# Third up-projection block: where its gate weights are loaded, when the SiLU table is loaded, and where the gating stands in the order

## The chip, the cores and the metric

The kernel runs on one core of one Trainium2 chip. A core has TensorE (PE; its weight loads are shown as PEld), VectorE (DVE), ScalarE (ACT), GpSimd (POOL) and SyncE (SP), which issues most DMAs. Each engine runs its own instructions in order and waits on semaphores for the others. The metric is the device time in microseconds of one execution, as the median of several runs; lower is better.

## The reference

One transformer-like layer on 1024 latent tokens of width 1024 with 256 context tokens: modulated RMSNorm, one input projection, retention and differential attention side by side, one output projection with a gated residual, then the part that matters here:

```python
h2 = rms_norm(x, norm2_g) * (1.0 + sc2) + sh2
x = x + g2 * conv_ffn(h2, w_up, conv_w, conv_b, w_down)

def conv_ffn(h, w_up, conv_w, conv_b, w_down):
    u = h @ w_up                                   # (1024, 2 * 2816)
    up = jnp.pad(u, ((0, 0), (1, 1), (0, 0)))
    u = up[:, :-2] * conv_w[0] + up[:, 1:-1] * conv_w[1] + up[:, 2:] * conv_w[2] + conv_b
    a, b = jnp.split(u, 2, axis=-1)
    return (jax.nn.silu(a) * b) @ w_down
```

## The kernel before, in words

All matrix products are made in float32 of about full precision: each operand is split into a high and a low part (`split_op`, L916: ACT casts the high part `whi` at L919, DVE subtracts to get the low part `wlo` at L920), and each 128x128x512 product is three matmuls, high x high (L129), high x low (L130) and low x high (L131).

The hidden width 2816 is worked off in 22 blocks of 128 columns (`NF`). Block j needs two weight blocks, `w_up[j]` (tile `wra`, the part that goes through the SiLU) and `w_up[j + 22]` (tile `wrb`, the gate weights), each 512 KB. The two weight blocks and the tokens form a 2x2 block product by a Strassen-like scheme with seven products, p1 to p7, of 12 matmuls each. POOL forms the sums of weight blocks (`combined`, L1064: L1074 adds two halves of `wrb`, L1075 to L1077 go on with `wra`), and the sums of activations, `B11`, `B21`, `B22`, `T1` to `T4`, are kept in SBUF. Some results are running sums in one PSUM bank, `chain`: p1, then p6 is added and ACT copies the bank (L1161), then p7 is added and ACT copies it (L1169), then p4 is added and ACT copies it (L1177). TensorE can't add the next product to the bank before the copy is made.

The order of the work around the change:

- In the output projection (L993 to L1018) `norm2` (L949) stores each of the 8 tiles `x1[t]`, sums its squares on ACT (L952), takes the power on POOL (`rsqrt`, L115) and scales the tile on DVE (L954). After it the tiles are turned by TensorE (`turned`, L959) and split into the activations; `turned1` (L1030) does the second half of the tokens and the sums beside the first products of the up-projection, and uses x1[4] to x1[7] for the last time.
- Products that need no sum of all activations come first (L1084 to L1099): p1 and p2 of blocks 0 to 2 (`NPRE`), p5 and p3 of blocks 0 and 1 (`NSUM`; the weight sums of these two blocks are made in place earlier).
- Then the main loop (L1187). In round j it loads the weights of block j + 1 (from block 3 on), calls `begin` (p1 and p2, or what is there of them), `end` of block j - 1 (p3 and p4), `gated` of block j - 1, and `middle` of block j (p6, p5, p7). `gated` (L1179) makes the width-3 convolution of both halves (`conv`, L1109: one ACT step at L1112 and two DVE steps at L1113 and L1114 each), the SiLU on ACT (L1182), the product with the gate on DVE (L1183) and the sums and stores for the down-projection (`down_operands`, L1121).
- Block 2 is the first whose weights are loaded in this part: `up_load(2)` (L977, called at L1118) loads `wrb` into a tile of its own, `third_b`, which takes memory over what `raw0` and the scratch tiles of `turned1` held, and then `wra` into one of the two buffers that the loads share. `in_order` (L117) fixes the order of the two.
- A scheduler orders the instructions of each engine by their place in the program and by when it reckons them ready; `add_manual_dep` with NoSync fixes an order between two instructions of one engine and adds no semaphore. A tile's memory is given on when all accesses to it are done.

The table of the SiLU is loaded by an instruction that the compiler puts ahead of the first activation that needs it.

Of the kernel before, what the change touches and what calls it, by code (L numbers as in the profile page):

```python
# [8 lines left out]
F32 = mybir.dt.float32  # L9
F32R = mybir.dt.float32r  # L10
BF16 = mybir.dt.bfloat16
AF = mybir.ActivationFunctionType
# [5 lines left out]
P = 128  # L18
D = 1024
KD = D // P  # L20
L = 1024
NT = L // P
# [6 lines left out]
NF = DFF // P  # L29
# [43 lines left out]
def kernel(  # L73
# [16 lines left out]
    nc = tc.nc  # L90
# [22 lines left out]
    def rsqrt(out_ap, in_ap, mul, eps, n):  # L113
        nc.vector.tensor_scalar(out=out_ap, in0=in_ap, scalar1=mul, scalar2=eps, op0=ALU.mult, op1=ALU.add)  # L114
        nc.gpsimd.tensor_tensor(out=out_ap, in0=out_ap, in1=mhalf[:, :n], op=ALU.pow)  # L115

    def in_order(start):  # L117
        last = {}
        for ins in nc.cur_bb.bb.instructions[start:]:
            if ins.engine not in FORCE:  # L120
                continue
            if ins.engine in last:
                tc.add_manual_dep(ins, last[ins.engine].name, mybir.DependencyInfo(mybir.DependencyClass.NoSync, mybir.DependencyReason.DATA), reason="order")
            last[ins.engine] = ins

    def passes(ps, lt, rt, first, last, more=False):
# [25 lines left out]
    with ExitStack() as p1:  # L152
# [217 lines left out]
        side = {"g": iter(()), "rate": 0.0, "due": 0.0}  # L370
# [7 lines left out]
        def beside(g, rate, due=0.0):  # L378
            for _ in side["g"]:
                pass  # L380
            side.update(g=g, rate=rate, due=due)
# [115 lines left out]
        with ExitStack() as p0:  # L497
# [92 lines left out]
            for i in range(2):  # L590
                for q in range(2):
                    t = 2 * i + q
# [287 lines left out]
    with ExitStack() as p2:  # L880
# [3 lines left out]
        start = len(nc.cur_bb.bb.instructions)  # L884
        order = sorted(TAU.items(), key=lambda it: it[1] % 1.0)
        for n in range(n_units + 8):
# [6 lines left out]
            if n in (8, 10, 12, 14):  # L893
                a, i = divmod(n // 2 - 4, 2)
# [8 lines left out]
            if n + 3 < n_units:  # L903
                after = units[n - 5].pool_ins if n >= 5 else last_va[0]
# [7 lines left out]
    wst = ctx_r.enter_context(tc.tile_pool(name="wst", bufs=2, side="right"))  # L912
# [7 lines left out]
        nc.vector.tensor_tensor(out=lo, in0=src, in1=r32(hi), op=ALU.subtract)  # L920
        return hi, lo

    def raw_load(name, src, pool=None):
        o = (pool or wst).tile([P, KD, P], F32, name=name)
        nc.sync.dma_start(out=o, in_=src)
        return o

    def product(ps, op, tt, first):
        hi, lo = op
        for k in range(4):  # L930
            passes(ps, (hi[:, k, :], lo[:, k, :]), (tt[0][:, k, :], tt[1][:, k, :]), first and k == 0, k == 3, not first)
            tick()

    B11, B21, B22, T1 = [tuple(yT[a][i][:, c : c + 4, :] for a in range(2)) for i, c in ((0, 0), (0, 4), (1, 0), (1, 4))]
    rawp = ExitStack()
    x1hp = rawp.enter_context(tc.tile_pool(name="x1h", bufs=1, side="right"))
    rwp = rawp.enter_context(tc.tile_pool(name="rwp", bufs=1, side="right"))
# [2 lines left out]
    x1lS = ExitStack()  # L940
    x1lp = x1lS.enter_context(tc.tile_pool(name="x1l", bufs=1, side="right"))
    xo = x1lS.enter_context(tc.tile_pool(name="xo", bufs=1, side="right"))
    x1 = [(x1lp if t < 4 else x1hp).tile([P, D], F32, name=f"x1_{t}") for t in range(NT)]
    raw0 = rwp.tile([P, KD, 512], F32, name="raw0")
    sm2 = rwp.tile([P, 64], F32, name="sm2")
    for t in range(NT):
# [2 lines left out]
    def norm2(t):  # L949
        nc.sync.dma_start(out=x1_d[t], in_=x1[t])  # L950
        sq = xo.tile([P, D], BF16, name="sq2")
        nc.scalar.activation(sq, x1[t], AF.Square, accum_out=sm2[:, t : t + 1])  # L952
        rsqrt(sm2[:, t : t + 1], sm2[:, t : t + 1], 1.0 / D, EPS, 1)
        nc.vector.tensor_scalar(out=x1[t], in0=x1[t], scalar1=sm2[:, t : t + 1], scalar2=None, op0=ALU.mult)  # L954

    def turned(hf, d, raw, on_act):
# [19 lines left out]
    NSUM = 2  # L976
    def up_load(j):  # L977
        if j == NSUM:
            start = len(nc.cur_bb.bb.instructions)
            b = raw_load("wrb", w_up[j + NF], third_b)  # L980
            a = raw_load("wra", w_up[j])
            in_order(start)
            return a, b
        return raw_load("wra", w_up[j]), raw_load("wrb", w_up[j + NF])

    def sums_in_place(a, b):
# [6 lines left out]
    with ExitStack() as p3:  # L993
        ps = p3.enter_context(tc.tile_pool(name="ps3", bufs=2, space=PSUM))
        for n in range(2):
# [3 lines left out]
            for t in range(NT):  # L999
# [5 lines left out]
                gated = wo.tile([P, 512], F32, name="gated")  # L1005
                nc.vector.tensor_tensor(out=gated, in0=pt, in1=g1[:, n * 512 : (n + 1) * 512], op=ALU.mult)
                nc.vector.tensor_tensor(out=dst, in0=gated, in1=dst, op=ALU.add)
                if n == 1:
                    norm2(t)
                    if t == 1:  # L1010
                        pre = [raw_load("wra" if j < 2 else "wrb", w_up[j]) for j in range(NPRE)]
                        early = [[split_op(a[:, c : c + 4, :]) for c in (0, 4)] for a in pre]
                        raws = [up_load(j) for j in range(NSUM)]
# [41 lines left out]
    def bank(name, pool=None):  # L1055
        return (next(bank_cycle) if pool is None else pool).tile([P, 512], F32, name=name, tag="bank")
# [40 lines left out]
    for j, pool in enumerate((psB, psC)):  # L1097
        third[j] = bank("third", pool)
        product(third[j], split_ahead[NSUM + j], B22, True)  # L1099
    beside(iter(()), 0.0)  # L1100
    tmpS.close()
    rawp.close()
    bank_cycle = itertools.cycle([psC] * 2 + [psB] * 2 + [psA] * 4)
# [2 lines left out]
    with ExitStack() as p4:  # L1106
        up = p4.enter_context(tc.tile_pool(name="up", bufs=2, side="right", reuse_waits="tile"))

        def conv(u, idx):  # L1109
            w = [cl[:, COL_CW + i * 44 + idx : COL_CW + i * 44 + idx + 1] for i in range(3)]  # L1110
            t = up.tile([P, L], F32, name="tconv", bufs=4)
            nc.scalar.activation(t, u, AF.Identity, scale=w[1], bias=cl[:, COL_CB + idx : COL_CB + idx + 1])  # L1112
            nc.vector.scalar_tensor_tensor(out=t[:, 1:], in0=u[:, : L - 1], scalar=w[0], in1=t[:, 1:], op0=ALU.mult, op1=ALU.add)  # L1113
            nc.vector.scalar_tensor_tensor(out=t[:, : L - 1], in0=u[:, 1:], scalar=w[2], in1=t[:, : L - 1], op0=ALU.mult, op1=ALU.add)  # L1114
            return t

        third_b = p4.enter_context(tc.tile_pool(name="third_b", bufs=1, side="right", reuse_waits="tile"))
        raws.append(up_load(NSUM))  # L1118
        held = {}

        def down_operands(j, g):  # L1121
            m, odd = divmod(j, 2)
            lo, hi = g[:, :512], g[:, 512:]
            eng = nc.gpsimd if j >= NF - 2 else nc.sync
            eng.dma_start(out=a_d[0][m][:, odd, :], in_=lo)
            if not odd:
                s34 = up.tile([P, 2, 512], F32, name="s34", bufs=1)
                nc.vector.tensor_tensor(out=s34[:, 0, :], in0=lo, in1=hi, op=ALU.subtract)
                held.update(lo=lo, hi=hi, s34=s34)
                return  # L1130
            eng.dma_start(out=a_d[3][m // 2][:, m % 2, :], in_=hi)
            s21 = up.tile([P, 2, 512], F32, name="s21", bufs=1)
            nc.vector.tensor_tensor(out=s21[:, 1, :], in0=held["hi"], in1=hi, op=ALU.add)
            nc.vector.tensor_tensor(out=s21[:, 0, :], in0=s21[:, 1, :], in1=held["lo"], op=ALU.subtract)
            eng.dma_start(out=a_d[1][m], in_=s21)
            nc.vector.tensor_tensor(out=held["s34"][:, 1, :], in0=lo, in1=s21[:, 0, :], op=ALU.subtract)
            eng.dma_start(out=a_d[2][m], in_=held["s34"])

        class Block:
# [18 lines left out]
            def middle(self):  # L1158
                j = self.j
                product(self.chain, self.op("p6"), T2, False)  # L1160
                nc.scalar.copy(self.ua[:, 512:], self.chain)  # L1161
                if j < NSUM:
                    self.third, self.fifth = third[j], fifth[j]
                    nc.vector.tensor_tensor(out=self.ua[:, 512:], in0=self.fifth, in1=self.ua[:, 512:], op=ALU.add)
                else:
                    self.third = self.fifth = bank("third")
                    product(self.third, self.op("p5"), T1, True)
                product(self.chain, self.op("p7"), T3, False)
                nc.scalar.copy(self.ub[:, 512:], self.chain)  # L1169
                nc.vector.tensor_tensor(out=self.ub[:, 512:], in0=self.fifth, in1=self.ub[:, 512:], op=ALU.add)  # L1170
# [5 lines left out]
                nc.vector.tensor_tensor(out=self.ua[:, 512:], in0=self.third, in1=self.ua[:, 512:], op=ALU.add)  # L1176
                nc.scalar.copy(self.ub[:, :512], self.chain)  # L1177

            def gated(self):  # L1179
                ta = conv(self.ua, self.j)  # L1180
                tb = conv(self.ub, self.j + NF)
                nc.scalar.activation(ta, ta, AF.Silu)  # L1182
                nc.vector.tensor_tensor(out=ta, in0=ta, in1=tb, op=ALU.mult)  # L1183
                down_operands(self.j, ta)

        last = None
        for j in range(NF):  # L1187
            if NSUM < j + 1 < NF:
                raws.append(up_load(j + 1))
            blk = Block(j)  # L1190
            blk.begin()
            if last is not None:
                last.end()
                last.gated()
            blk.middle()
            last = blk
        last.end()

# [6 lines left out]
        def split1(src):  # L1205
            hi, lo = split_op(src.rearrange("p (a b) -> p a b", b=P))
            return flat(hi), flat(lo)

        def step(pd, a, b, first, last, more=False, ts=range(4)):
            for t in ts:  # L1210
                passes(pd[t], tuple(g[:, t * P : (t + 1) * P] for g in a), b, first, last, more)
# [3 lines left out]
        for m in range(2):  # L1215
# [5 lines left out]
            for i, cc in enumerate((c1, c2)):  # L1221
                step(cc, split1(pa[:, i * C : (i + 1) * C]), split1(pb[:, i * C : (i + 1) * C]), m == 0, False)
        last.gated()
    ctx_t.close()
    ctx_y.close()
    ctx_ya.close()
# [218 lines left out]
```

## Time and profile before

| | |
|---|---|
| median of 3 runs | 1414.38 us (1412.52 to 1414.53) |
| span of the profiled execution, first to last instruction | 1413.6 us (the page gives no other time of it) |
| TensorE busy | 1372.1 us, 97% of the span |
| DVE busy | 991.1 us, 70% |
| ACT busy | 729.1 us, 52% |
| POOL busy | 286.1 us, 20% |
| mean granted TensorE clock | 0.992 |
| TensorE waits between 740 and 860 us | 4.6 us in three waits |

Times in the rows are microseconds from the span's start. A timeline row has the start, the duration, the engine, the line, the operation, output<-inputs, the shape and a count; brackets at its end hold the idle time of the engine ahead of it and what ended that idle time. In the table of windows each row has the stretch, its length, and the busy time with the number of instructions of PE, PEld, DVE, ACT and POOL, then the granted clock of TensorE (1.00 is full speed), the share of time that the DMA engines were busy, and GB/s. A row of waits has who waited for whom, the total, how often, and the longest. The up-projection runs from about 760 to 1190 us.

### The profile page before, as it was taken

To read this page: it belongs to the slowest core of one execution; us is meant where nothing else is said; L and a number is where in the kernel's file an instruction comes from. 1 tells how busy PE (TensorE), PEld (TensorE's weight loads), DVE (VectorE), ACT (ScalarE), POOL (GpSimd) and SP (SyncE) were. 2 spreads that over 40 slices of the span, in tenths; PEclk is the share of its full clock that TensorE was granted. 3 is DMA by queue.
4 is the path that set the end of the run, shared out by engine and by line. 5 is a ranking of instruction groups with operands and counts; after the bars stand their busy time and mean duration, and the time that the engine had idled before them with its cause. 6 is when DMAs were issued, how large, how long until landed. Compare 5 with 4: busy or idle time off the path is not lost.

```text
span 1413.6 us, 19193 instructions
## 1 busy us (share of the span) xinstructions
PE 1372.1 (97%) x6924; PEld 1141.8 (81%) x6924; DVE 991.1 (70%) x1433; ACT 729.1 (52%) x1386; POOL 286.1 (20%) x321
## 2 busy tenths in 40 slices
PE   6999999999999999999999999999999999999996
PEld 2588888888888799998888778888888888888885
DVE  3464965334586798896357888877788777898457
ACT  3453312333565689997126645554455555455533
POOL 1220000000556133411201232233322220000001
PEclk8999999999999999999999999999999999999999
DMA  8645886365474796631421223223233226953224
GB/s 305 228 135 179 280 293 202 116 201 183 149 246 159 196 220 153 128 79 62 163 82 60 90 105 112 92 109 112 97 112 112 81 84 221 393 180 105 90 97 178
DMA packets 96662, 218.79 MB, mean 155 GB/s; under 512 B 9204, under 2 KB 31220, under 8 KB 96056
## 3 DMA queue, kind: packets, MB, share of 16 engines
q1 hardware_dynamic: 88408, 192.67, 39.3%
q0 software_dynamic: 8160, 24.91, 7.8%
q8 instruction: 54, 0.88, 0.2%
q14 instruction: 40, 0.33, 0.1%
HBM read 160.13 MB, written 57.41 MB: 154 GB/s over the span
## 4 chain that ended last, share of the span: by engine, by line
PE 81%; DMA 5%; issue 5%; DVE 4%; POOL 2%; ACT 2%; SPq 0%; POOLq 0%; DVEq 0%; ACTq 0%
PE pA L748 5%; PE pv L780 5%; PE chain L129 5%; PE chain L130 5%; PE chain L131 5%; PE c L131 4%; PE c L129 4%; PE c L130 4%; PE pn L130 3%; PE pn L129 3%; PE pn L131 3%; PE pl L129 3%; PE pl L131 3%; PE pl L130 3%; PE third L129 2%
## 5 line engine op out<-in xcount | busy, mean ns | idle before, releaser
L129 PE MATMUL chain<-T,whi 128*128 128x512 f32 x264 | 104.2, 395 | 4.7 <-ACT ua L1161 3.9
L129 PE MATMUL pl<-hT,whi 128*128 128x512 f32 x256 | 106.2, 415 | 0.0
L130 PE MATMUL chain<-T,whi 128*128 128x512 f32 x264 | 104.1, 394 | 0.0
L131 PE MATMUL chain<-T,wlo 128*128 128x512 f32 x264 | 103.9, 394 | 0.0
L131 PE MATMUL pl<-hT,wlo 128*128 128x512 f32 x256 | 100.2, 391 | 0.0
L130 PE MATMUL pl<-hT,whi 128*128 128x512 f32 x256 | 100.0, 391 | 0.0
L751 DVE TENSOR_REDUCE mt<-pA 128x1 f32<-128x1280 f32 x64 | 95.3, 1490 | 3.6 <-PE pA L748 2.1
L131 PE MATMUL c<-whi,ghl 128*128 128x512 f32 x232 | 90.4, 390 | 0.2 <-DVE ghl L1245 0.2
L748 PE MATMUL pA<-ks,qhl 128*128 128x512 f32 (+1 forms) x384 | 89.4, 369 | 1.0 <-ACT p L755 1.0
L130 PE MATMUL c<-wlo,ghl 128*128 128x512 f32 x232 | 90.3, 389 | 0.0
L129 PE MATMUL c<-whi,ghl 128*128 128x512 f32 x232 | 90.2, 389 | 0.0
L755 ACT ACTIVATE p<-pA,mt 128x1280 f32<-128x1280 f32 x64 | 85.5, 1337 | 6.7 <-DVE mt L751 4.5
L919 ACT CAST whi<-cmb 128x512 fp32r<-128x512 f32 x62 | 38.6, 623 | 86.4 <-PE chain L130 66.9
L129 PE MATMUL pn<-whi,hT 128*128 128x512 f32 x192 | 78.2, 408 | 0.0
L748 PEld LDWEIGHTS pA<-ks,qhl 128*128 128x128 f32 x384 | 67.6, 189 | 13.0 <-ACT p L755 1.4
L1074 POOL TENSOR_TENSOR cmb<-wrb 128x512 f32<-128x512 f32 x20 | 27.2, 1361 | 248.0 <-DMA wrb<-w_up 180.1
L780 PE MATMUL pv<-va,aT 128*128 128x128 f32 x640 | 77.0, 275 | 0.1
L130 PE MATMUL pn<-wlo,hT 128*128 128x512 f32 x192 | 76.1, 396 | 0.0
L131 PE MATMUL pn<-whi,hT 128*128 128x512 f32 x192 | 75.1, 394 | 0.5 <-DVE hT L552 0.5
L920 DVE TENSOR_TENSOR wlo<-cmb,whi 128x512 fp32r<-128x512 f32 x62 | 58.5, 946 | 23.1 <-ACT whi L919 23.1
L780 PEld LDWEIGHTS pv<-va,aT 128*128 128x128 f32 x640 | 74.0, 192 | 0.7 <-DVE yT L809 0.3
L115 POOL TENSOR_TENSOR sm<-sm,mhalf 128x1 f32<-128x1 f32 x26 | 16.1, 621 | 279.3 <-DVE sm L114 279.2
(302 smaller groups left out, 3809.3 us busy)
## 6 DMA issues: line engine op xcount, KB each, us to landing
wm<-w_mod SPq DMA_DIRECT2D x32, 512.0 KB, 5.4
raw<-w_in SPq DMA_DIRECT2D x28, 512.0 KB, 4.7
wra<-w_up SPq DMA_DIRECT2D x24, 512.0 KB, 3.3
wrb<-w_up SPq DMA_DIRECT2D x23, 512.0 KB, 3.5
W<-w_down SPq DMA_DIRECT2D x44, 256.0 KB, 6.0
ad<-s SPq DMA_DIRECT2D x20, 512.0 KB, 3.6
wra<-ad SPq DMA_DIRECT2D x20, 512.0 KB, 3.3
kvs<-kvg SPq DMA_DIRECT2D x36, 256.0 KB, 2.9
```

The costliest lines, as they stand in the source:

```text
L115: nc.gpsimd.tensor_tensor(out=out_ap, in0=out_ap, in1=mhalf[:, :n], op=ALU.pow)
L129: mm(ps, lh, rh, start=first, stop=False, skip_group_check=more)
L130: mm(ps, lh, rl, start=False, stop=False, skip_group_check=more)
L131: mm(ps, ll, rh, start=False, stop=last, skip_group_check=more)
L748: mm(self.pa[m][:, c0:c1], self.q[:, m, i, qs], self.k[:, m, c0:c1], start=(i == 0), stop=(i == 1))
L751: nc.vector.tensor_reduce(out=self.mt[:, m : m + 1], in_=self.pa[m][:, :LK], axis=AX.X, op=ALU.min)
L755: nc.scalar.activation(self.p[m], self.pa[m][:, :LK], AF.Exp, scale=-1.0, bias=self.mt[:, m : m + 1], accum_out=self.s[:, m : m + 1])
L780: mm(self.pv, self.aT[:, c, :], self.v[:, c, :], start=(c == 0), stop=(c == NKT - 1))
L919: nc.scalar.copy(hi, src)
L920: nc.vector.tensor_tensor(out=lo, in0=src, in1=r32(hi), op=ALU.subtract)
L1074: nc.gpsimd.tensor_tensor(out=s1, in0=b1, in1=b2, op=ALU.add)
```

## The change

Three edits go together.

1. The last of the eight `x1` tiles gets a pool of its own, `x1k`, that stays open to the end of the up-projection. The gate weights of block 2 are loaded into this tile instead of `third_b`, which is gone. `up_load(2)` is called earlier in the program, right after the first products, and the forced order of its two loads is gone; `wrb` is issued first.
2. In `norm2(0)` a SiLU of one column into an unused column of `sm2` is added, so that the table is loaded there.
3. In rounds 1 to 3 of the main loop, `gated` of the block before is called after `middle` instead of before it, and its SiLU is ordered behind the copy at L1161 of that `middle` on ACT (`order_only`). `gated` of blocks 3 and later stands where it stood.

```diff
+    def order_only(ins, before):
+        tc.add_manual_dep(ins, before.name, mybir.DependencyInfo(mybir.DependencyClass.NoSync, mybir.DependencyReason.DATA), reason="order")
...
-    def raw_load(name, src, pool=None):
-        o = (pool or wst).tile([P, KD, P], F32, name=name)
+    def raw_load(name, src, o=None):
+        o = wst.tile([P, KD, P], F32, name=name) if o is None else o
         nc.sync.dma_start(out=o, in_=src)
...
+    keptp = ctx.enter_context(ExitStack())
+    x1k = keptp.enter_context(tc.tile_pool(name="x1k", bufs=1, side="right", reuse_waits="tile"))
...
-    x1 = [(x1lp if t < 4 else x1hp).tile([P, D], F32, name=f"x1_{t}") for t in range(NT)]
+    x1 = [(x1lp if t < 4 else x1hp).tile([P, D], F32, name=f"x1_{t}") for t in range(NT - 1)]
+    x1.append(x1k.tile([P, D], F32, name="x1_7"))
...
         rsqrt(sm2[:, t : t + 1], sm2[:, t : t + 1], 1.0 / D, EPS, 1)
+        if t == 0:
+            nc.scalar.activation(sm2[:, 32:33], sm2[:, 0:1], AF.Silu)
...
         if j == NSUM:
-            start = len(nc.cur_bb.bb.instructions)
-            b = raw_load("wrb", w_up[j + NF], third_b)
-            a = raw_load("wra", w_up[j])
-            in_order(start)
-            return a, b
+            b = raw_load("wrb", w_up[j + NF], x1[NT - 1].rearrange("p (k l) -> p k l", k=KD))
+            return raw_load("wra", w_up[j]), b
...
     beside(iter(()), 0.0)
+    raws.append(up_load(NSUM))
     tmpS.close()
     rawp.close()
...
-        third_b = p4.enter_context(tc.tile_pool(name="third_b", bufs=1, side="right", reuse_waits="tile"))
-        raws.append(up_load(NSUM))
...
-                nc.scalar.copy(self.ua[:, 512:], self.chain)
+                self.copied = nc.scalar.copy(self.ua[:, 512:], self.chain)
...
-            def gated(self):
+            def gated(self, after=None):
                 ta = conv(self.ua, self.j)
                 tb = conv(self.ub, self.j + NF)
-                nc.scalar.activation(ta, ta, AF.Silu)
+                silu = nc.scalar.activation(ta, ta, AF.Silu)
+                if after is not None:
+                    order_only(silu.ins, after.ins)
...
         for j in range(NF):
+            late_gate = 0 < j < 4
             if NSUM < j + 1 < NF:
                 raws.append(up_load(j + 1))
             blk = Block(j)
             blk.begin()
             if last is not None:
                 last.end()
-                last.gated()
+                if not late_gate:
+                    last.gated()
             blk.middle()
+            if late_gate:
+                last.gated(blk.copied)
             last = blk
...
         last.gated()
+    keptp.close()
```

More of the change, by code (lines that the diff above doesn't have):

```diff
@@ L122, in in_order @@
             if ins.engine in last:
-                tc.add_manual_dep(ins, last[ins.engine].name, mybir.DependencyInfo(mybir.DependencyClass.NoSync, mybir.DependencyReason.DATA), reason="order")
+                order_only(ins, last[ins.engine])
             last[ins.engine] = ins
```

## The prediction

> **What bounds the kernel now.** I read the page's span first, then who TensorE (PE) waits for, then the granted clock in narrow windows, then the timelines of ACT, POOL, SyncE (SP) and DVE around each wait. "p1" to "p7" are the seven products of a block (12 matmuls each), "j0" the block.
>
> ```profile
> span 1413.6 us, 19193 instructions
> PE 1372.1 (97%) x6924; PEld 1141.8 (81%) x6924; DVE 991.1 (70%) x1433; ACT 729.1 (52%) x1386; POOL 286.1 (20%) x321
> ```
>
> The three runs have a median of 1414.38, 0.8 above the span; what lies outside the span isn't touched, so I subtract from the median. TensorE is busy 97%, so only its idle time and its clock can be won. The waits of TensorE, from 740 to 860 us (first two rows) and from 845 to 1400 (last row):
>
> ```profile
> PE chain L129 <- ACT ua L1161: 3.9, 2, 2.1
> PE chain L129 <- ACT ub L1169: 0.7, 1, 0.7
> ...
> PE c L131 <- DVE ghl L1245: 0.2, 1, 0.2
> ```
>
> Three waits make 4.6 us; behind them TensorE runs without a wait to the last stage, so what is won there arrives at the end one for one. The second loss is the clock. These windows have PE busy first and PEclk after POOL:
>
> ```profile
> 802.64:806.06 3.42, 1.56 (x7) 0.97 (x7) 2.26 (x4) 3.41 (x5) 2.56 (x3) 1.00 0.47 153
> 806.06:809.47 3.41, 3.41 (x10) 2.66 (x9) 3.41 (x4) 2.33 (x4) 0.46 (x1) 0.50 0.00 0
> 836.78:840.19 3.41, 1.33 (x7) 0.89 (x6) 3.38 (x4) 2.57 (x4) 0.00 (x0) 1.00 0.16 62
> 840.19:843.60 3.41, 3.41 (x10) 2.63 (x9) 2.77 (x4) 0.27 (x1) 0.00 (x0) 0.50 0.44 164
> ```
>
> After each of the two long waits the clock is 0.50 for 3.41 us: 1.7 us of work lost each time. The 0.7 us wait has no such stretch behind it. So at most 0.73 + 1.85 + 1.7 + 2.08 + 1.7 = 8.06 us are to be had, with the single waits read here (idle time and its releaser in brackets):
>
> ```profile
> 799.60 0.50 PE L129 MATMUL chain<-T,whi 128*128 128x512 f32 x1 [0.73 <-ACT ub L1169]
> ...
> 805.17 0.50 PE L129 MATMUL chain<-T,whi 128*128 128x512 f32 x1 [1.85 <-ACT ua L1161]
> ...
> 839.12 0.50 PE L129 MATMUL chain<-T,whi 128*128 128x512 f32 x1 [2.08 <-ACT ua L1161]
> ```
>
> Each is a product that adds to a PSUM bank which ACT must copy first. ACT runs in order, and its rows show what stood ahead of the copies:
>
> ```profile
> 798.44 0.62 ACT L919 CAST whi<-cmb 128x512 fp32r<-128x512 f32 x1 [0.77 <-POOL cmb L1075]
> 798.97 0.58 ACT L1169 COPY ub<-chain 128x512 f32<-128x512 f32 x1
> ...
> 801.80 1.28 ACT L1182 ACT_TABLE_LOAD   x1 [1.74 <-DVE tconv L1114]
> 803.10 1.06 ACT L1182 ACTIVATE tconv<-tconv 128x1024 f32<-128x1024 f32 x1
> 804.06 0.57 ACT L1177 COPY ub<-chain 128x512 f32<-128x512 f32 x1
> 804.52 0.59 ACT L1161 COPY ua<-chain 128x512 f32<-128x512 f32 x1
> ...
> 837.54 1.06 ACT L1182 ACTIVATE tconv<-tconv 128x1024 f32<-128x1024 f32 x1 [1.63 <-DVE tconv L1114]
> 838.50 0.57 ACT L1161 COPY ua<-chain 128x512 f32<-128x512 f32 x1
> ```
>
> First a cast that waits for POOL, then the SiLU with its table load, then a SiLU that waits for DVE.
>
> **Part 1, the load.** POOL and SP rows of the third block (j2):
>
> ```profile
> 795.74 1.29 POOL L1074 TENSOR_TENSOR cmb<-wrb 128x512 f32<-128x512 f32 x1 [30.84 <-DMA wrb<-w_up]
> 797.11 1.29 POOL L1075 TENSOR_TENSOR cmb<-cmb,wra 128x512 f32<-128x512 f32 x1
> SPq L925 <- DVE T L967: 30.1, 1, 30.1
> 719.74 42.21 SPq L950 DMA_DIRECT2D x1d<-x  x8
> 792.05 0.33 SPq L925 DMA_DIRECT2D wrb<-w_up  x1
> 792.48 1.71 SPq L925 DMA_DIRECT2D wra<-w_up  x2
> wrb<-w_up SPq DMA_DIRECT2D x23, 512.0 KB, 3.5
> 779.02 0.60 PE L959 MATMUL pt<-ident,x 128*128 128x128 f32 x4
> ```
>
> The wrb load waits 30.1 us for the last split that reads the memory under its buffer. In the last x1 tile it waits only for the last transposes (779.02 + 0.60), so it is issued near 779.7 and lands near 783.2. SP has nothing else between the x1 stores and 792: nobody is queued behind it but wra of the same block, which keeps its own wait (its buffer is read by the split at 790.69 below). wra therefore lands near 795.8 and L1075 starts 1.3 us earlier than 797.11. That takes the cast out of the way of L1169: **0.73 us won**. The number of loads is unchanged.
>
> The price: L1074 moves to about 783, beside a DVE that has no gap.
>
> ```profile
> 782.00:796.00 14.00, 14.00 (x63) 11.29 (x62) 13.97 (x24) 7.24 (x13) 0.26 (x1) 1.00 0.20 75
> 763.61 1.29 POOL L1071 TENSOR_TENSOR cmb<-wrb,wra 128x512 f32<-128x512 f32 x1
> 763.71 1.74 DVE L920 TENSOR_TENSOR wlo<-wrb,whi 128x512 fp32r<-128x512 f32 x1 [0.70 <-ACT whi L919]
> 790.69 0.70 DVE L920 TENSOR_TENSOR wlo<-wra,whi 128x512 fp32r<-128x512 f32 x1
> 791.44 0.19 PEld L131 LDWEIGHTS chain<-T,wlo 128*128 128x128 f32 x1
> ```
>
> DVE is busy 13.97 of 14.00 us. Beside a POOL addition the same split took 1.74 instead of 0.70, so the move costs DVE 0 to 1.3 us, and I take 1.04. The split at 790.69 ends at 791.39 and TensorE loads its result at 791.44: no slack. So TensorE stalls there: **1.04 us lost**, a new wait. Below nothing it can't go, since nothing leaves DVE's queue. The Trainium skill, SBUF — State Buffer, "SBUF: two separate sides", says that a GpSimd instruction and a DVE instruction with two SBUF inputs take a shared port pair as an exclusive lock for the whole instruction. The two rows agree; by that rule the loss would be at most one POOL duration, 1.3, and the time 0.3 later than mine.
>
> **Part 2, the table.** ACT and POOL near the first norm2:
>
> ```profile
> 721.21 0.55 POOL L115 TENSOR_TENSOR sm<-sm,mhalf 128x1 f32<-128x1 f32 x1 [27.33 <-DVE sm L114]
> 725.24 1.06 ACT L952 ACTIVATE sq<-x 128x1024 bf16<-128x1024 f32 x1 [4.30 <-DVE x L1007]
> ```
>
> The preload waits for POOL until 721.76 and needs 1.28 plus a one-column activation (0 to 1.06; I take 0.2). ACT's next work starts at 725.24, so 2 us of cover remain: it costs nothing. Were the cover gone, the squares would be late by under 1 us, with nobody waiting near them. It takes 1.28 us out of the queue ahead of the copy at 804.52.
>
> **Part 3, the order.** The SiLU of j0, j1, j2 now waits in ACT's queue for L1161 of the next block. For the wait at 805.17, table load and SiLU (2.34 us) leave the way, but TensorE's last pass before it (802.92) belongs to the product that is to be copied, so a copy and its hand-over stay: 804.52 to 805.17 is 0.65, plus 0.05. 1.85 becomes 0.70: **1.15 won**, and as no long idle is left in one window, **1.7** of clock. For 839.12 there are 2.7 us of another product (p5) under the copy, so all of it goes: **2.08 + 1.7 won**. The Trainium skill, TensorE: Matmul & The Clock Gate, "What's actually happening", throttles after about 3.4 us idle. The trace differs: 1.85 was enough, and a rival below has the time by that rule.
>
> What waits for the later SiLU is L1183 on DVE, with splits queued behind it, and later the store of the gate on SP:
>
> ```profile
> 811.04 1.22 DVE L1183 TENSOR_TENSOR tconv<-tconv 128x1024 f32<-128x1024 f32 x1
> 812.17 1.28 DVE L1113 SCALAR_TENSOR_TENSOR tconv<-ua,cl,tconv 128x1023 f32<-128x1023 f32 x1
> 813.97 1.28 DVE L1114 SCALAR_TENSOR_TENSOR tconv<-ua,cl,tconv 128x1023 f32<-128x1023 f32 x1
> ...
> 818.92 1.78 DVE L920 TENSOR_TENSOR wlo<-wra,whi 128x512 fp32r<-128x512 f32 x1
> 820.76 0.19 PEld L131 LDWEIGHTS chain<-yT,wlo 128*128 128x128 f32 x1
> ```
>
> The SiLU of j0 would be done at 804.52 + 0.59 + 1.06 = 806.2, five before L1183: the added wait costs nothing. What is late next is DVE itself. The split for p1 of j3 ends at 820.70 and is loaded at 820.76. TensorE now comes there 0.73 + 1.15 + 1.7 - 1.04 = 2.5 us earlier. DVE can follow, since the copies it waits for come earlier too, but not wholly: 0 to 2.5 lost, I take **0.5**, near the end at which DVE follows, because its idle waits before 816 are all for ACT.
>
> **Sum.** 8.06 - 1.04 - 0.70 - 0.5 = 5.8 us: 1414.4 - 5.8 = **1408.6**.
>
> **Rivals.** *All of it* (0.15): POOL finds a gap and the scheduler puts another product under the copy at 805: 8.06 won, 1406.3. For it: L1161's product could be followed by one of j2. Against it: the full DVE.
>
> *Another wait in the SiLU's place* (0.14): with the SiLU gone, the in-order ACT takes a convolution's first step (L1112, of the size of the 1.06 and 1.28 us steps quoted; I take 1.25) ahead of L1161 of j1. Then 0.70 + 1.25 = 1.95 idle, and the clock falls again: 8.06 - 1.04 - 1.95 - 1.7 - 0.5 = 2.9 won, 1411.5. For it: that step is ready as soon as L1177 ends.
>
> *It does not do what it says* (0.13): beside that other wait, the one at 839 returns with its clock (3.78), because L1161 of j3 again stands behind L1112 or behind a SiLU that waits for DVE. 8.06 - 1.04 - 1.95 - 1.7 - 3.78 = 0.4 lost, 1414.8. For it: the DVE that this SiLU waits for is no faster than before.
>
> *The clock doesn't hang on these waits* (0.03): both stretches of 0.50 come all the same, and 5.8 - 3.4 = 2.4 is won, 1412.0. Against it: both begin within 1.1 us of the end of a long wait, and none comes without one. (The rule of the clock page of the Trainium skill, cited above, asks for longer idle times than these.)
>
> *Slower* (0.10): one mechanism, on DVE ahead of the split for p1 of j3. A gating is two each of L1113 and L1114, L1183 and a half-width subtraction (half of L1183): 4 x 1.28 + 1.22 + 0.6 = 6.9 us. If the later gating of j0 slides in front of that split too, it ends at 827.6 instead of 820.70; TensorE waits about 9 us, and the clock falls (1.7). Against before: +6.9 + 1.7 - 3.8 (the wait at 839) = +4.8, 1419.2. It decides from a split end at 822.9 on: 4.6 us of stall and 1.7 of clock eat the 6.3 won elsewhere. Against it: DVE had four idle microseconds before 816.
>
> **The numbers.** The forecast has 0.45. Its own range is 1407 to 1410.5. To hold 8 in 10 the range goes from 1405.6 (all of it, less the spread of the runs) to 1414.2 (the other wait, the clock, and the near part of the case that does nothing); it leaves out the slower case and 0.08 of that one. Within 0.2% (2.8 us) is about what a measurement can't tell from no change. Faster by more: 0.45 + 0.15 + half of the 1411.5 case, which lies on that bound (0.07), = 0.67; same: 0.07 + 0.13 + 0.03 = 0.23; slower: 0.10.
>
> **What would show it.** The wrb load of j2 issued near 780 and L1074 near 783; a stall of about 1 us of TensorE at its first wlo of p6 of j0, with DVE's splits a microsecond late; no table load near 802; the wait at 805 at 0.7 and no clock of 0.50 after 800; no wait at p7 of j3. I am wrong if a table load appears in front of any later SiLU, if a wait of 1.8 us or more is left, or if TensorE stalls for wlo at p1 or p2 of j3 by over 2 us.

## The result, and the profile after

Twelve runs of the changed kernel have a median of 1414.61 us (1411.14 to 1418.16), beside 1415.39 for the kernel before: a ratio of 0.9995, 95% interval [0.9982, 1.0007]. A second set of twelve (the run r1_after below) gave 0.9986 [0.9975, 0.9997]. So the change brought nothing that can be told from no change, or very little; 1408.6 was forecast.

The page of the profiled execution (1413.53 us) begins:

```profile
span 1411.6 us, 19199 instructions
...
PE 1369.6 (97%) x6924; PEld 1140.4 (81%) x6924; DVE 994.9 (70%) x1433; ACT 729.5 (52%) x1387; POOL 298.0 (21%) x321
```

The waits of TensorE from 776 to 1300 us (who waited for whom, the total, how often, the longest):

```profile
PE c L132 <- ACT ghl L1255: 2.1, 1, 2.1
PE chain L132 <- ACT ub L1173: 1.4, 1, 1.4
PE c L134 <- DVE ghl L1256: 0.5, 1, 0.5
PE chain L132 <- ACT ua L1065: 0.4, 1, 0.4
PE chain L132 <- ACT ua L1165: 0.3, 1, 0.3
```

Of the waits of 1.85 and 2.08 for `ua`, 0.3 is left of the first and nothing of the second; one of 0.4 is new, at another copy into `ua` (L1065). The one for `ub`, 0.73 before, is now 1.4. And a pair for `ghl` is new, far away from the change: `ghl` is the split left operand of the down-projection. The windows of the changed kernel around 805, where the clock fell before, show 1.00 (the third number from the end), as those around 839 do:

```profile
802.40:805.80 3.40, 2.98 (x14) 2.14 (x13) 3.29 (x5) 0.86 (x2) 1.49 (x2) 1.00 0.88 300
805.80:809.20 3.40, 3.10 (x13) 2.23 (x13) 3.37 (x5) 3.40 (x6) 2.70 (x3) 1.00 0.02 8
```

I measure from TensorE's first `fifth` product, to leave out what stands ahead of it: that product starts between 776.7 and 782.5 in the profiles of this study, a spread larger than what the edits ahead of it could bring. The stretch from there to the first product of the down-projection (`c`) is A, and from that one to the end of the span is B. Each profile gives one execution. TensorE's rows of before:

```profile
780.16 0.39 PE L129 MATMUL fifth<-yT,whi 128*128 128x512 f32 x1
...
1186.30 0.39 PE L129 MATMUL c<-whi 128*128 128x512 f32 x1
```

and of the changed kernel:

```profile
781.21 0.40 PE L132 MATMUL fifth<-yT,whi 128*128 128x512 f32 x1
...
1181.73 0.39 PE L132 MATMUL c<-whi 128*128 128x512 f32 x1
```

A was 406.14 and is 400.52: **5.62 us are won where the change was made**; 5.8 were forecast. B was 1413.6 - 1186.30 = 227.3 and is 1411.6 - 1181.73 = 229.9: **2.6 us are lost behind it**, in a part of the program that no line of the diff names. These are TensorE's rows there:

```profile
1209.09 0.39 PE L134 MATMUL c<-whi,wlo 128*128 128x512 f32 x1
1211.55 0.50 PE L132 MATMUL c<-whi,ghl 128*128 128x512 f32 x1 [2.08 <-ACT ghl L1255]
...
1212.81 0.50 PE L134 MATMUL c<-whi,ghl 128*128 128x512 f32 x1 [0.53 <-DVE ghl L1256]
```

and this is what the chain that ended last shows just ahead of them (start, duration, what):

```profile
1201.76 8.63 DMA ad<-s
1210.39 0.03 ACTq L1255
...
1210.46 1.05 ACT ghl L1255
1211.53 1.24 DVE ghl L1256
```

The first `ghl` cast waits until a store of the last gating has read its tile. `ad<-s` stands for two stores, of the tiles `s21` and `s34`; this one is the later, of `s34` (L1141, issued at 1201.76). Here is ACT's row of that cast, and then its first two `ghl` casts before, where the first waited for no store but the second did:

```profile
1210.46 1.04 ACT L1255 CAST ghl<-wra 128x1024 fp32r<-128x1024 f32 x1 [5.47 <-DMA ad<-s]
...
1211.02 1.05 ACT L1244 CAST ghl<-wra 128x1024 fp32r<-128x1024 f32 x1 [1.42 <-DVE W L1249]
1214.93 1.05 ACT L1244 CAST ghl<-wrb 128x1024 fp32r<-128x1024 f32 x1 [2.86 <-DMA ad<-s]
```

Neither cast reads what the store writes. They meet in memory. These are the addresses in the two programs (KB of a partition, from the lowest address of the two `ghl` buffers, which is the same in both; `tconv` has four buffers, `tconv 3` and `tconv 4` are two of them):

| | 0-4 | 4-8 | 8-12 | 12-16 |
|---|---|---|---|---|
| up-projection, before | tconv 3 | tconv 4 | s34 | s21 |
| up-projection, changed | tconv 4 | s34 | s21 | x1_7 |
| down-projection, both | first ghl | first ghl | second ghl | second ghl |

Before, `x1_7` was freed with the other x1 tiles and the tiles of the gating were put at the top; the changed kernel keeps `x1_7` there, so that they slide down by 4 KB. At the end of the up-projection all of them are given up and `ghl` is put at the top again: its first buffer now lies over `s34`, whose store is the last of all.

**My theory**, then: the order of the SiLUs won what was forecast; the early load won nothing, and by moving the layout it gave about half back. **The first rival**: the transfers set the pace from 1190 to 1240, where the DMA share is about 1, so that TensorE's earlier arrival is lost there whatever the layout. **The second**: the POOL sum that the load moved costs DVE 1.04, as I had forecast, and the rest of the gain was never there.

### The profile page after: what moved, and what is told of

Its sections match the earlier page's. It is cut to its first block, busy times and chain, and to the rows that moved or that the text cites. A ratio compares the mean times of both kernels' runs of the same rounds, so it can differ in the third digit from the quotient of the medians.

```text
span 1411.6 us, 19199 instructions
## 1 busy us (share of the span) xinstructions
PE 1369.6 (97%) x6924; PEld 1140.4 (81%) x6924; DVE 994.9 (70%) x1433; ACT 729.5 (52%) x1387; POOL 298.0 (21%) x321
## 4 chain that ended last, share of the span: by engine, by line
PE 83%; DVE 6%; DMA 5%; issue 3%; POOL 2%; ACT 1%; SPq 0%; POOLq 0%; DVEq 0%; ACTq 0%
PE chain L133 5%; PE chain L132 5%; PE chain L134 5%; PE pA L751 5%; PE pv L783 5%; PE pn L132 4%; PE c L134 4%; PE pn L133 4%; PE c L133 4%; PE pn L134 4%; PE c L132 4%; PE pl L134 3%; PE pl L133 3%; PE pl L132 3%; PE third L133 3%
```

## The experiments

A and B are as above, from one profile of each; the ratio is that of the time to the kernel before, on the same chip from e1 on, with its 95% interval. The runs were made on several chips, so they are compared with each other only by these ratios. e6 and r2 were run once each and have no ratio.

| run | A | B | ratio |
|---|---|---|---|
| before | 406.1 | 227.3 | |
| after | 400.5 | 229.9 | 0.9995 [0.9982, 1.0007] |
| e1_layout | 400.5 | 227.9 | 0.9964 [0.9951, 0.9978] |
| e2_order_table | 400.1 | 227.9 | 0.9964 [0.9950, 0.9979] |
| e3_load | 407.8 | 231.4 | 1.0045 [1.0025, 1.0065] |
| e4_order | 400.3 | 227.0 | 0.9968 [0.9956, 0.9979] |
| e5_swap | 406.3 | 227.4 | 0.9995 [0.9984, 1.0006] |
| e6_quarters | 400.9 | 230.1 | |
| e7_swap | 406.2 | 229.0 | 1.0025 [1.0013, 1.0036] |
| e8_between | 401.4 | 226.9 | 0.9977 [0.9965, 0.9989] |
| e9_pad | 400.1 | 226.7 | 0.9966 [0.9954, 0.9977] |
| e10_conv | 400.3 | 227.9 | 0.9963 [0.9951, 0.9976] |
| r1_after | 400.5 | 231.1 | 0.9986 [0.9975, 0.9997] |
| r2_after | 400.5 | 229.3 | |

**e1_layout: the layout alone undone.**

```diff
         last.gated()
-    keptp.close()
     ctx_t.close()
```

> The changed kernel, except that the memory of the last x1 tile stays taken to the end, so that the two ghl buffers of the down-projection slide down by 4 KB and lie as before over (two tconv buffers) and (s34, s21), instead of over (tconv, s34) and (s21, x1_7). Nothing else moves; no instruction changes its place. Theory (layout): in the changed kernel the first ghl cast waited 5.47 us for the store that reads s34, the last one of the last gating, and TensorE lost 2.08 + 0.53 behind it; here both waits are gone, the 4.5 us that the changed kernel is ahead at 1185 arrive at the end: 1411.6 - 2.6 = 1409.0 by its span, a ratio to the kernel before of 0.9967. Rival (DMA): between 1190 and 1240 the transfers are busy at 1.0 and set the pace; then the waits stay whatever the layout, and the time is that of the changed kernel, 0.9995. The second ghl cast should then be the one that waits for ad<-s, with TensorE not behind it.

A stays and B falls by 1.9. The first cast comes at 1205.83 instead of 1210.46, held up only by a store that reads a tconv tile, and the second one waits for `ad<-s`, as before. ACT's rows:

```profile
1205.83 1.05 ACT L1254 CAST ghl<-wra 128x1024 fp32r<-128x1024 f32 x1 [1.68 <-DMA ad<-tconv]
1210.13 1.05 ACT L1254 CAST ghl<-wrb 128x1024 fp32r<-128x1024 f32 x1 [3.25 <-DMA ad<-s]
```

Of TensorE's waits for `ghl` one is left, for the second cast's low part:

```profile
PE c L134 <- DVE ghl L1255: 0.9, 1, 0.9
```

The ratio is 0.9964, beside the 0.9967 of the theory; the first rival gave 0.9995 and falls.

**e5_swap and e7_swap: the mirror image, in the kernel before.** A dummy tile was to make the two `ghl` buffers change places:

```diff
+            if (i, m) == (0, 4):
+                dop.tile([P, 2, 2 * C], F32R, name="ghl")
             o = dop.tile([P, 2, 2 * C], F32R, name="ghl")
```

> The kernel before, except that the two ghl buffers of the down-projection change places: the first cast goes into the one over s34 and s21, the second into the one over two tconv buffers. No instruction changes its place. Theory (layout): the first ghl cast, 1211.02 before, waits for the last store of the last gating and comes at about 1214.9; TensorE waits about 2.6 us there, as in the changed kernel, and the time is 1414.4 + 2.6 = 1417.0, a ratio of 1.0018. Rival (DMA, or the 4.5 us earlier arrival of TensorE at a fixed end of the transfers): nothing changes, ratio 1.000.

Nothing changed, ratio 0.9995: the unused tile got no address in the program, so the buffers stayed where they were. This run says nothing on the theory. With a pool for each buffer they do change places:

```diff
-        dop = p5.enter_context(tc.tile_pool(name="dop", bufs=2, side="right", reuse_waits="tile"))
+        dops = itertools.cycle([p5.enter_context(tc.tile_pool(name=f"dop{n}", bufs=1, side="right", reuse_waits="tile")) for n in range(2)])
...
-            o = dop.tile([P, 2, 2 * C], F32R, name="ghl")
+            o = next(dops).tile([P, 2, 2 * C], F32R, name="ghl")
```

> The kernel before, with the two ghl buffers of the down-projection as pools of their own, so that the first cast really goes into the one over s34 and s21 and the second into the one over two tconv buffers (in the run e5_swap the buffers kept their addresses, and its first cast did not wait). No instruction changes its place. Theory (layout): the first ghl cast waits for the last store that reads s34 or s21, till about 1215; TensorE waits 2 to 2.6 us there, with or without a stretch at half clock behind it (1.7): 1414.4 + 2.3 = 1416.7, up to 1418.5; ratio 1.0015 to 1.003. Rival (the transfers set the pace there, and the changed layout is chance): no wait, ratio 1.000.

ACT's first cast and the waits of TensorE that follow:

```profile
1213.85 1.04 ACT L1244 CAST ghl<-wra 128x1024 fp32r<-128x1024 f32 x1 [4.65 <-DMA ad<-s]
```

```profile
PE c L129 <- ACT ghl L1244: 1.3, 1, 1.3
PE c L131 <- DVE ghl L1245: 0.5, 1, 0.5
```

So the kernel before gets waits of the same kind (1.3 + 0.5) from two addresses alone, with every instruction in its place but for the semaphore waits, and TensorE arriving no earlier (A is 406.2 beside 406.1): 1.0025. That the buffer's place makes the wait is shown from both sides. (The ratio stands for 3.5 us, while B in this one profile is 1.7 longer. A stretch at half clock behind the wait in other executions could be the rest, but this execution has none, so that isn't shown.)

**e2_order_table and e4_order: the change without the load, then without the table preload too**. Against the changed kernel, e2 first and then what e4 takes away besides:

```diff
-    x1.append(x1k.tile([P, D], F32, name="x1_7"))
...
-            b = raw_load("wrb", w_up[j + NF], x1[NT - 1].rearrange("p (k l) -> p k l", k=KD))
+            b = raw_load("wrb", w_up[j + NF], third_b.tile([P, KD, P], F32, name="wrb"))
...
+        third_b = p4.enter_context(tc.tile_pool(name="third_b", bufs=1, side="right", reuse_waits="tile"))
+        raws.append(up_load(NSUM))
```

```diff
-        if t == 0:
-            nc.scalar.activation(sm2[:, 32:33], sm2[:, 0:1], AF.Silu)
```

> The change without its first part: the third block's gate weights are loaded as before into a pool of their own, so up, s34 and s21 lie where they lay before; the SiLU table is preloaded and the SiLUs stand behind the copies. Theory (the order gives all, the load nothing, the layout takes back): the two long waits and both stretches at half clock go, POOL's first sum stands at about 796 and takes 1.3 us again, there are no new waits at 1211, and the time is 5 to 5.6 below before: 1409.1, a ratio of 0.9963. My forecast's view (the load is worth 0.73 less 1.04) gives about the same 5.8 + 0.3 = 6.1 or 0.9957, so the POOL row decides between these two. Rival (the gain is lost to the transfers at 1190 to 1240): 0.9995 as in the changed kernel.

> The order of the SiLUs alone, without the early load and without the table preload. Theory (the order gives all): the SiLU with its table load (2.3 us) stands behind the copies, so the table load delays nobody: the time is that of order and table together, 0.9964, within 0.7 us. Rival (the preload is worth its 1.28 us): 1.3 us slower than those two together, 0.9973, with a wait that grows by about that behind the table load near 806.

Both are where e1 is. The order alone makes the whole gain, and the early load adds nothing to it: A is 400.1 and 400.3 without it, 400.5 with it. The preload is worth nothing that can be seen: in e4 the table load stands behind the copies that TensorE waits for, as ACT's rows show:

```profile
802.02 0.59 ACT L1164 COPY ua<-chain 128x512 f32<-128x512 f32 x1
802.50 1.25 ACT L1115 ACTIVATE tconv<-ub,cl 128x1024 f32<-128x1024 f32 x1
803.77 1.28 ACT L1185 ACT_TABLE_LOAD   x1
```

**e3_load: the load alone.** Against the changed kernel, besides the preload's two lines:

```diff
-            late_gate = 0 < j < 4
+            late_gate = False
```

> The first part of the change alone: the early load into the last x1 tile, no table preload, no order of the SiLUs. Theory: POOL's first sum of the third block starts near 783 and takes some 13 us beside a DVE without a gap, so nothing is won near 799 (0 to 0.9 us); the waits of 1.85 and 2.08 with their half clock stay; at the first ghl cast the s34 store is waited for as in the changed kernel and TensorE loses 2.6: the time is 1414.4 + 1.7 to 2.6 = 1416.6, a ratio of 1.0015. Rival, my forecast's step: the sum takes 1.3 to 2 us and holds DVE up by 1.04, TensorE stalls for that at the first wlo of p6 of the first block and wins 0.73 at 799: 1414.7 without a loss at the ghl cast.

The run is slower than the theory and the rival said, 1.0045. TensorE's waits from 776 to 1300:

```profile
PE chain L132 <- ACT ua L1163: 5.2, 2, 3.1
PE c L132 <- ACT ghl L1253: 2.0, 1, 2.0
PE chain L132 <- ACT ub L1171: 1.5, 1, 1.5
PE c L134 <- DVE ghl L1254: 0.5, 1, 0.5
```

The wait at 805 grew from 1.85 to 3.1 and the one at 799 from 0.73 to 1.5, so without the new order the early load costs 1.6 us in A as well. And behind the wait for `ghl` the clock fell for one stretch (the second row):

```profile
1217.25:1220.67 3.42, 1.16 (x4) 0.68 (x5) 1.70 (x2) 2.78 (x4) 0.00 (x0) 1.00 1.04 410
1220.67:1224.08 3.41, 3.41 (x10) 2.64 (x9) 3.41 (x6) 1.29 (x3) 0.00 (x0) 0.50 1.05 409
```

That is B: 2.0 + 0.5 of waits and 1.7 of clock make the 4.1 that it is longer, to 0.1. The DVE rival's stall at the first `wlo` of p6 is not among the waits, so the second rival falls too.

**e6_quarters: what held POOL up.** In the changed kernel POOL's sum started early as forecast, and took ten times its 1.29 us:

```profile
784.07 13.17 POOL L1079 TENSOR_TENSOR cmb<-x 128x512 f32<-128x512 f32 x1 [18.07 <-DVE yT L975]
```

In this run it is cut into four:

```diff
-        nc.gpsimd.tensor_tensor(out=s1, in0=b1, in1=b2, op=ALU.add)
+        for c in range(4) if j == NSUM else ():
+            nc.gpsimd.tensor_tensor(out=s1[:, c, :], in0=b1[:, c, :], in1=b2[:, c, :], op=ALU.add)
+        if j > NSUM:
+            nc.gpsimd.tensor_tensor(out=s1, in0=b1, in1=b2, op=ALU.add)
```

> The changed kernel, with POOL's first sum of the third block (512 elements per partition) cut into four instructions of 128 each. Theory (POOL is shut out while DVE works without a gap, by the whole instruction): the first quarter takes about 12 us, from 784 to the first idle time of DVE near 796, and the other three some 0.35 each. Rival 1 (it works on, at about a tenth of its rate): four quarters of about 3.3 us each. Rival 2 (it gets a turn between two instructions of DVE): the quarters take under 1.5 us each and the sum is done before 790; then it could have been of use, and the next sum, which waits for wra landing near 796, still comes no earlier.

The view of the tile `cmb` (shortest, median and longest of the four in ns) and POOL's row up to 791:

```profile
L1080 POOL TENSOR_TENSOR cmb<-x x4: 452/456/12380, 779.5 to 792.7; 128x128 f32<-128x128 f32 x4
```

```profile
779.51 12.38 POOL L1080 TENSOR_TENSOR cmb<-x 128x128 f32<-128x128 f32 x1 [18.02 <-DMA x<-w_up]
```

One quarter takes 12.38 us and the others 0.45: POOL doesn't work slowly there, it is shut out. The first one ends at 791.89, so its own 0.45 us began at 791.44. DVE's rows there:

```profile
790.89 0.68 DVE L923 TENSOR_TENSOR wlo<-wrb,whi 128x512 fp32r<-128x512 f32 x1
791.49 0.68 DVE L1171 TENSOR_TENSOR ua<-fifth,ua 128x512 f32<-128x512 f32 x1
```

The theory had DVE go idle there, and it did not. What ended was a run of instructions with two SBUF inputs, one every 0.60 us; the one at 791.49 reads `fifth` from PSUM. In each of the seven profiles with the early load POOL's own work (1.29, here 0.45) begins 0.03 to 0.06 us ahead of that DVE instruction. No run moves the instruction, so that it is what lets POOL in rests on these times alone. DVE lost nothing: its spacing is 0.60 throughout. The Trainium skill, SBUF — State Buffer, "SBUF: two separate sides", says that a DVE instruction with two SBUF inputs and a GpSimd instruction that reads SBUF exclude each other from a shared port pair, and that the one that comes second blocks fully. The 12.38 and the place where it ends agree. That the pair goes to the one that starts first is to be read with care: POOL's sum waited through some twenty starts of DVE.

**e8_between: a product of another chain over each copy.** Against e2; `sixth` is p6 and its copy, taken out of `middle`:

```diff
             blk.begin()
+            if 0 < j <= NSUM:
+                blk.sixth()
...
+            if not 0 < j <= NSUM:
+                blk.sixth()
             blk.middle()
```

> The change without its early load (order and table, 0.9964), and in the second and third block the sixth product goes ahead of the fourth product of the block before, so that each copy of a chain has a product of another chain over it. Theory: the two waits that are left there (0.79 at 799 and 0.80 at 808) go, nothing else changes: 1.6 us below that, ratio 0.9953. Rival: a split or a copy is late in the new order and a wait of another kind comes in their place: 0.9964 or above.

The two waits of e2, 0.8 each, gave way to others, from 776 to 850:

```profile
PE chain L132 <- ACT ua L1165: 1.0, 1, 1.0
PE chain L134 <- DVE wlo L923: 0.7, 1, 0.7
PE chain L132 <- ACT ub L1176: 0.4, 1, 0.4
```

A is 1.3 longer than in e2, of which these waits account for 0.5, and the ratio is 0.9977: the rival held. Where the other 0.8 went isn't known.

**e9_pad: both ghl buffers over tconv.** Against e4:

```diff
     with ExitStack() as p5:
+        p5.enter_context(tc.tile_pool(name="pad", bufs=1, side="right")).tile([P, 2 * D], F32, name="pad")
```

> The order of the SiLUs alone (0.9968), and 8 KB left free before the down-projection's tiles, so that both ghl buffers lie over tconv buffers and neither over s34 or s21. No instruction changes its place. Theory (layout): no ghl cast waits for the last two stores any more; the second cast, which waited 3.25 us for ad<-s where the buffers lay as before, comes up to 3 us earlier. TensorE waited there for the second cast's low part by 0.9 us at most or not at all, so the time gains 0 to 0.9: 0.9962 to 0.9968. Rival: wra and wrb themselves land late in the busy transfers, and nothing changes in the profile either.

No cast waits for a store any more, ACT's first two rows:

```profile
1201.82 1.04 ACT L1254 CAST ghl<-wra 128x1024 fp32r<-128x1024 f32 x1
1202.77 1.05 ACT L1254 CAST ghl<-wrb 128x1024 fp32r<-128x1024 f32 x1
```

B is the shortest of all, by 0.2 beside e8 and 0.3 beside e4; the time, 0.9966, is not to be told from e1, e2, e4 and e10. All five are faster than the kernel before, and all five ratios lie below both of the changed kernel (0.9995 and 0.9986), though their intervals just touch that of the second. e4, a change of a few lines, is the simplest.

**e10_conv: the convolution behind the copy.** Against e1; `act` is the activation that opens `conv`:

```diff
-                nc.scalar.copy(self.ub[:, 512:], self.chain)
+                self.seventh = nc.scalar.copy(self.ub[:, 512:], self.chain)
...
-                ta = conv(self.ua, self.j)
+                ta = conv(self.ua, self.j, self.seventh if self.j == 0 else None)
...
+            if after is not None:
+                order_only(act.ins, after.ins)
```

In the changed kernel ACT's rows ahead of that copy are:

```profile
798.65 0.62 ACT L922 CAST whi<-cmb 128x512 fp32r<-128x512 f32 x1 [2.84 <-POOL cmb L1080]
799.17 1.24 ACT L1118 ACTIVATE tconv<-ua,cl 128x1024 f32<-128x1024 f32 x1
800.32 0.60 ACT L922 CAST whi<-cmb 128x512 fp32r<-128x512 f32 x1
800.82 0.57 ACT L1173 COPY ub<-chain 128x512 f32<-128x512 f32 x1
```

> The changed kernel with the old layout of the ghl buffers (0.9964), and the convolution's first step of the first block ordered behind the copy of the seventh product's chain. Theory: in the changed kernel that 1.24 us step stood ahead of the copy at 800.82 and made the wait of TensorE there 1.44 instead of 0.73; behind the copy it no longer does, the wait falls to about 0.7 and the time by about 0.7: 0.9959. Rival: the cast that waits for POOL, ahead of both, sets the copy's start; then the wait stays at 1.4.

With the step behind the copy, the wait there falls from the 1.5 of e1 to 0.3, so the convolution step made it grow. But a wait of 0.8 for `ua` stands where 0.3 stood, A is 0.2 shorter, and the time is 0.9963: no gain that can be measured.

**r1_after and r2_after: the changed kernel again.**

> The changed kernel once more, to see how the wait at the first ghl cast goes from execution to execution, and what the time is beside another set of runs of before. Theory: the wait of 2.08 + 0.53 comes in each execution, since the layout makes it; the granted clock behind it is 1.00 in some and 0.50 for one stretch in others, as it was behind the same wait with the early load alone, which costs 1.7 us. From the first product of the fifth kind to the end the profile then shows 630.4 (as before) or 632.1; the time is between 1.7 below and 1 above before, ratio 0.998 to 1.000. Rival: the wait is chance and is missing in this execution: 628 and a ratio near 0.9965.

> The changed kernel, a second look beside the one above. Theory: the same wait of about 2.1 and 0.5 at the first ghl cast, with the clock behind it at 1.00 or, for one stretch, 0.50. Rival: no wait.

The wait for `ghl` is there each time, with 1.7 + 0.5 and 1.5 + 0.5 (and 2.2 + 0.5 in e6, which has the same layout). In r1_after the clock falls behind it:

```profile
1211.33:1214.74 3.41, 1.76 (x6) 1.16 (x7) 2.31 (x3) 3.39 (x5) 0.00 (x0) 1.00 1.04 411
1214.74:1218.15 3.41, 3.41 (x9) 2.63 (x8) 3.41 (x7) 1.29 (x3) 0.00 (x0) 0.50 1.03 405
```

and B is 231.1; in r2_after it does not, and B is 229.3. So a run of the changed kernel loses 2 to 3.8 us in B against before, of the 5.6 won in A. Over the profiles this leaves 1.8 to 3.6, while the two ratios stand for 0.7 and 2.0 (-1.0 to 3.5 by their intervals); how many of the runs without a profile had the stretch at half clock isn't known.

## Why the prediction was wrong

The step that failed is the sentence "what is won there arrives at the end one for one". It was read from the one row in which TensorE waited for `ghl` by 0.2 us after 845. That row says that nobody was late in the layout of before; it can't say so of another layout. Part 1 was priced as a load that moves in time. That a tile kept longer moves every tile below it, and what then comes to lie over what, had no term in the sum: it costs 2.6 us of waits (2.08 + 0.53), and 1.7 more when the clock falls, as it did in two of the five profiles that have the load and this layout (e3 and r1). One of the signs of being wrong that the prediction names, a wait of 1.8 us or more, came here.

Ahead of the down-projection the sum came out, 5.8 against 5.62, but only in part for its reasons. What the order of the SiLUs wins was right. The other terms, +0.73 for the load, -1.04 on DVE and -0.5 on DVE, make -0.81, and in their place stands a wait that grew by 0.71: three wrong terms with nearly the right sum, which is luck. (These waits and the clock make 5.9, of which the 5.62 leave 0.3 unaccounted for.)

Point by point:

- **Part 1, "0.73 us won".** Wrong. The load was issued at 780.72, as forecast, but POOL's first sum ended at 784.07 + 13.17 = 797.24; before, it ended at 795.74 + 1.29 = 797.03 in an execution that stood 1.05 us earlier here. So the cast that waits for POOL gained 0.84 us instead of 1.3, it still stands ahead of the copy, and with a convolution step and a second cast between them the wait grew to 1.4. This is the step of about 1.25 us that the prediction's second rival named, ahead of another copy than it said.
- **"1.04 us lost" on DVE, "below nothing it can't go".** Wrong: the row that showed a split at 1.74 beside POOL had POOL ahead. In a dense run of DVE it is POOL that waited, 12 us, and no split was late.
- **Part 2.** Right, it costs nothing (the table load and its SiLU end at 723.53, ACT's next work starts at 726.32); and e4 shows that it brings nothing either, once the order is there.
- **Part 3, 0.70 left at 805, nothing at 839, no half clock.** Right for the whole: 0.3 is left at that copy, 0.4 is new at the copy of L1065, nothing is left at 839, and 3.4 of clock is won. The order makes A 5.9 shorter alone (e4) and 6.0 with the table preload (e2).
- **0.5 on DVE at p1 of j3.** Too high: no wait for `wlo` shows in the list.
- **The rivals.** None was the one that came. "It does not do what it says" had the right time, 1414.8, by the wrong mechanism: it let the wait at 839 return with its clock, and it did not.

## What to carry to other kernels

A tile that is kept longer, or put elsewhere, shifts every tile that is placed after it, so price such an edit by two lists: what becomes late in time, and which later tile now lies over a tile that something still reads. Where a store is the last reader of a buffer, let the next user of that memory be the one that needs it last. And a TensorE wait of nearly nothing in the old profile is no proof of slack: ask which of the casts and loads behind it had a wait of its own that was just covered, as the second `ghl` cast here.

## What the runs showed of the hardware

- A POOL addition of 1.29 us took 13.17 beside a run of DVE instructions with two SBUF inputs, each 0.60 apart, and got its turn as the first DVE instruction that reads PSUM came up (e6 and six more profiles).
- Waits of TensorE of like length did and did not bring a stretch at half clock: 1.69 + 0.53 did in r1_after, and the 2.08 at 839 in the kernel before did. The changed kernel's own profile had 2.08 + 0.53 where r1_after had its waits, and kept 1.00, as e3 did behind one of 2.08 that ended at 843.64:

```profile
1207.98:1211.39 3.41, 1.49 (x7) 0.91 (x5) 0.00 (x0) 0.93 (x1) 0.00 (x0) 1.00 1.05 412
1211.39:1214.80 3.41, 2.72 (x11) 1.96 (x12) 3.27 (x4) 3.14 (x6) 0.00 (x0) 1.00 1.03 406
```

  From 780 to 1400 us the half-clock stretches are 3.41 long (one of e3 is two of that), and within a profile they lie on one grid of that length: those of before begin at 806.06 and 840.19, ten lengths apart. In the length of the grid ahead of each drop TensorE was busy for 1.13 to 1.76 us of the 3.41. The clock stayed at 1.00 behind two lengths with 1.56 (e3) and 1.57 (the changed kernel, whose grid lies 0.08 ahead of the rows above), and behind every length at full clock with 1.80 or more. The Trainium skill, TensorE: Matmul & The Clock Gate, "What's actually happening", speaks of a free-running window of activity, which this grid agrees with; a wait could then count by how it falls on the windows. Between 1.56 and 1.76 the busy time alone doesn't decide it, and no run here settles what does.
